# Three moves in a gated attention and recurrence block: an order written out for TensorE, eight copies on another engine, one unit's weight sums later

## The chip, the cores and the metric

The kernel runs on one core of a Trainium2 chip. The metric is the device time of one execution in microseconds (us), as the median of several runs. The profile is of one further execution, recorded by the hardware profiler. A core has a matrix engine, TensorE (PE), with its weight loads shown apart as PEld; VectorE (DVE), ScalarE (ACT) and GpSimd (POOL) for elementwise work; and SyncE (SP), which here only issues transfers. Each engine works through its own instructions in order, and waits at an instruction until what it needs is there.

## The reference

One layer, for 512 frames of 1024 values, in float32:

```python
xn = rmsnorm(x, norm_mix_g)
q, k, v, xr, gr, ga, gb = split(xn @ w_in)
ya = chunked_band_attention(q, k, v, rel_table) @ w_attn_out   # 16 heads of 64
yb = (rg_lru(causal_conv(xr)) * gelu(gr)) @ w_rnn_out
g_a, g_b = split(sigmoid([ga, gb] + b_merge))
h = x + (g_a * ya + g_b * yb) @ w_o
hn = rmsnorm(h, norm_ffn_g)
g, up = split(hn @ w_ffn_in)                                   # 2 x 2816 columns
h = h + (silu(g) * up) @ w_ffn_out
out = rmsnorm(h, final_norm_g)
```

The attention of a head adds a learned bias to the scores of earlier chunks, takes a softmax over them, and multiplies by v.

## The kernel before

**Matrix products.** A float32 operand is split into a high part, which ACT writes rounded to the matrix engine's type, and a low part, which DVE writes as the difference (`split`, lines 82 and 83). A product is then three matmuls (`mm3`, lines 76 to 78): high by high, high by low, low by high. Weights arrive by transfers that SP issues (`raw_...`, line 147) and are split into `whl_...`.

**Products by seven instead of eight.** Large products are grouped in units, in which sums and differences of weight blocks stand for one of eight block products. The sums of the blocks of w_ffn_out and w_o are made early, and parked in device memory: `spill` (lines 586 to 596) loads four blocks, makes four subtractions on DVE, the first line 591, and stores the results. `spill_of` does it for a unit, with buffers from a given pool. Unit 3's sums are made inside the loop over heads, after head 5 (`if h == 5`), in buffers of the pool `rnp`.

**Order.** The framework's scheduler chooses each engine's order from the program and from estimated costs, except in sections that `manual_schedule` covers for PE: there PE follows the program as written. The loop over heads is such a section. The stretch from the plain tiles of w_o to the first FFN tiles is not.

**Attention.** `scores` (lines 686 to 712) makes a head's scores (s), DVE adds the bias and takes the row extreme (line 707), ACT makes the exponentials with their row sums (708), DVE inverts the sums (`rl`, 709), POOL scales the four tiles of probabilities p (711). PE transposes p in the next step of the head loop (722) and uses it (742). POOL also casts the keys' low part, `kl` (656).

**After the attention.** The `ya` loop multiplies the attention's output by w_attn_out in eight tiles, `po_ya0` to `po_ya7`, 24 matmuls each; two tiles share one pair of weight loads, `raw_ya`, and splits, `whl_ya`.

**The plain tiles of w_o and the FFN norm.** Eight tiles `po_h` (four blocks t of 128 frames, two halves cc of the columns) get their last products in a loop over t. After each, DVE adds it into h (line 933) and ACT squares it for the norm (935). `norm_half` (339 to 360) then takes two blocks t: it scales them (`xs`, line 345), has PE transpose them in groups of two columns' tiles (`pt_ffn`, line 353), and writes from each transposed tile the high part `hn` (ACT, 357), the low part (DVE, 358) and a float copy `x` (ACT, 360), which later sums need. `first` are the first four FFN tiles, `po_f0` to `po_f3`, from the weights `fg0` and `fu0`; `project_half` makes one half of the frames of one of them. `weight_sums` prepares sums of FFN weights (`s_fg`, `s_fu`) and their splits on the same engines in the same stretch.

Of the kernel before, what the change touches and what calls it, by code (L numbers as in the profile page):

```python
# [36 lines left out]
def block_kernel(ctx: ExitStack, tc: tile.TileContext, x, norm_mix_g, w_in, b_merge, rel_table,  # L37
# [3 lines left out]
    pe, dve, act, pool, sp = nc.tensor, nc.vector, nc.scalar, nc.gpsimd, nc.sync  # L41
# [26 lines left out]
    def f(ap):  # L68
        return ap.bitcast(F32)

    def mm_tile(name, tag="mm"):
        return ps.tile([P, S], F32, tag=tag, bufs=4 if tag == "mm" else 2, name=name)

    def mm3(o, sh, sl, mh, ml, start, stop, parts=False):

        pe.matmul(o, sh, mh, start=start, stop=False, skip_group_check=parts)  # L76
        pe.matmul(o, sh, ml, start=False, stop=False, skip_group_check=parts)  # L77
        pe.matmul(o, sl, mh, start=False, stop=stop, skip_group_check=parts)  # L78
# [49 lines left out]
    front, units = (0, 1, 10), ((2, 3), (4, 5), (6, 7), (8, 9))  # L128
# [116 lines left out]
    def weights(name, ahead=1):  # L245
        prefetch(index[name] + 1 + ahead)
        return made[index[name]]
# [58 lines left out]
    ident = cp.tile([P, P], F32, name="ident")  # L306
# [3 lines left out]
    warm = cp.tile([P, 1], F32, name="warm")  # L310
# [28 lines left out]
    def norm_half(pl, src, ssq, g, dst, half, name, whole_of=None, then=None):  # L339
        xs = []  # L340
        for i in range(2):
            t = 2 * half + i
            rs = rstd(ssq[t], f"{name}{t}")
            xsc = pl.tile([P, D], F32, tag="xs", bufs=2, name=f"xs_{name}{t}")
            dve.tensor_scalar(xsc[:], src[t][:], rs[:, 0:1], None, ALU.mult)
            xs.append(xsc)
        if then:
            act.activation(warm[:], rs[:], then)
        for jp in range(0, KT, 2):
            pt = ps.tile([P, 2, 256], F32, tag="t", bufs=2, name=f"pt_{name}{half}_{jp}")  # L350
            for i in range(2):
                for j in range(2):
                    pe.transpose(pt[:, j, i * P:(i + 1) * P], xs[i][:, (jp + j) * P:(jp + j + 1) * P], ident[:])
            for j in range(2):
                jj = jp + j
                hi, lo = dst(jj, 0, half), dst(jj, 1, half)
                act.activation(hi, pt[:, j], AF.Identity, scale=g[:, jj:jj + 1])  # L357
                dve.scalar_tensor_tensor(lo, pt[:, j], g[:, jj:jj + 1], f(hi), ALU.mult, ALU.subtract)
                if whole_of:
                    act.activation(whole_of(jj, half), pt[:, j], AF.Identity, scale=g[:, jj:jj + 1])  # L360

    def features(pl, tag, name):

# [222 lines left out]
    def spill(w, unit, to, r):  # L586

        for n in range(4):
            sp.dma_start(out=r[n], in_=square(w, unit[n // 2], n % 2))
        b11, b12, b21, b22 = r  # L590
        dve.tensor_sub(b11, b12, b11)
# [190 lines left out]
    with tc.manual_schedule(engines={mybir.EngineType.PE}):  # L782
        for h in range(HEADS):
            pp = transposed(h, prob)
            if h + 1 < HEADS:
                prob = scores(h + 1)
            before, after = laid[h].split("|")
            project_all(before)
            weigh(h, pp)
            project_all(after)  # L790
            if h == 5:
                r = [rnp.tile([P, 2, 2, S], F32R, tag="big", bufs=4, name=f"spill3_{n}") for n in range(2)]
                spill(w_ffn_out, units[3], sums_d[3], [f(t[:, i]) for t in r for i in range(2)])
    aw2_stack.close()
    wo_stack, wop = opened("wo", 4)

# [39 lines left out]
    for j in range(KT):  # L836
        if j >= 4:
            wo_part(*blocks_wo[j - 4])
        py = mm_tile(f"po_ya{j}")
        project(py, weights(f"ya{j - j % 2}"), j % 2, aT)  # L840
        dve.scalar_tensor_tensor(ta[j], ta[j], 1.0, py[:], ALU.add, ALU.mult)
        dve.tensor_add(ta[j], ta[j], zB[j])
        at = lo_half if j < 2 else slice(0, S)
        split(mT[j][:, 0, at], mT[j][:, 1, at], ta[j][:, at])
        if j == 3:
            m_sum("s1")
            m_split("s1", m32("22"), m_at(0, hi_half))
            for name in ("s2", "s4", "s3"):
                m_sum(name)
# [66 lines left out]
    def hn_at(k, part, half):  # L916
        return bl[k // 4, half][:, part, k % 4]
# [1 line left out]
    hsq = []  # L919
    act.activation(warm[:], eps_t[:], AF.Sqrt)  # L920
    weight_sums("fg2", True)
    for t in range(NT):
        q2 = cp.tile([P, 2], F32, tag="hsq2", bufs=2, name=f"hsq2_{t}")
        for cc in range(2):
            po = bank_of(t, cc)
            for i in (2, 3):
                w = wo[f"wo{i}_{cc}"]
                for k in range(2):
                    mk = mT[2 * i + k]
                    mm3(po[:], mk[:, 0, t * P:(t + 1) * P], mk[:, 1, t * P:(t + 1) * P], w[:, 0, k], w[:, 1, k],  # L930
                        (t > 1 and cc == 1) and i == 2 and k == 0, k == 1, parts=True)
            hs = ht[t][:, cc * S:(cc + 1) * S]
            dve.scalar_tensor_tensor(hs, po[:], 0.5, hs, ALU.mult, ALU.add)
            junk = tg_.tile([P, S], F32, tag="tg", name=f"hj{t}_{cc}")
            act.activation(junk[:], hs, AF.Square, accum_out=q2[:, cc:cc + 1])
        q = cp.tile([P, 1], F32, tag="ssq", bufs=4, name=f"hsq{t}")
        dve.tensor_reduce(q[:], q2[:], mybir.AxisListType.X, ALU.add)
        hsq.append(q[:])
        if t == 1:
            norm_half(x32p, ht, hsq, gf, hn_at, 0, "ffn", f_at)  # L940
    wo_stack.close()
    xn_stack.close()

# [16 lines left out]
    def project_half(o, whl, c, half):  # L960
        at = slice(c * P, (c + 1) * P)
        for k in range(KT):
            mm3(o[:, half * 256:half * 256 + 256], whl(0, k, at), whl(1, k, at),
                hn_at(k, 0, half), hn_at(k, 1, half), k == 0, k == KT - 1)

    first = [mm_tile(f"po_f{i}") for i in range(4)]
    for i, name in enumerate(("fg0", "fg0")):
        project_half(first[i], weights(name), i % 2, 0)
    norm_half(x32p, ht, hsq, gf, hn_at, 1, "ffn", f_at, AF.Silu)
    for i, name in enumerate(("fu0", "fu0")):  # L970
        project_half(first[2 + i], weights(name, 0), i % 2, 0)


    def sums(name):
        t = acp.tile([P, 4, 256], F32, tag="act", name=f"sum_{name}")
# [28 lines left out]
    prefetch(index["fg2"] + 1)  # L1004

    for i, name in enumerate(("fg0", "fg0", "fu0", "fu0")):
        project_half(first[i], weights(name, 0), i % 2, 1)
    act0 = act_tile(0)
    for c in range(2):
        tg = swiglu_gate(first[c], c)  # L1010
# [239 lines left out]
```

## Time and profile before

| what | value |
|---|---|
| runs | 870.02, 870.34, 869.25 us; median 870.02 |
| profiled execution | 871.76 us, of which span 869.9 |
| PE busy | 852.9 us, 98% |
| DVE, ACT, POOL busy | 620.0, 505.3, 103.0 us |
| mean granted TensorE clock | 0.995 |
| the unit sums' loads (line 589) | 16, landing after 2.7, 5.8, 9.5 us (least, median, most) |

The span is from the first to the last instruction; the execution's time is 1.9 us longer. A row of a timeline gives the start, the length, the engine, the line and the operation, its result and its operands, and in brackets how long the engine idled before it and what ended the idling. A matmul's length overlaps the next one's: what counts is the distance between starts. A row of windows gives each engine's busy time in a stretch, and the granted clock as a share of full speed.

### The profile page before, as it was taken

To read this page: it belongs to the slowest core of one execution; us is meant where nothing else is said; L and a number is where in the kernel's file an instruction comes from. 1 tells how busy PE (TensorE), PEld (TensorE's weight loads), DVE (VectorE), ACT (ScalarE), POOL (GpSimd) and SP (SyncE) were. 2 spreads that over 40 slices of the span, in tenths; PEclk is the share of its full clock that TensorE was granted. 3 is DMA by queue.
4 is the path that set the end of the run, shared out by engine and by line. 5 is a ranking of instruction groups with operands and counts; after the bars stand their busy time and mean duration, and the time that the engine had idled before them with its cause. 6 is when DMAs were issued, how large, how long until landed. Compare 5 with 4: busy or idle time off the path is not lost.

```text
span 869.9 us, 12990 instructions
## 1 busy us (share of the span) xinstructions
PE 852.9 (98%) x4908; PEld 747.2 (86%) x4908; DVE 620.0 (71%) x952; ACT 505.3 (58%) x870; POOL 103.0 (12%) x135
## 2 busy tenths in 40 slices
PE   8999999999999998999999999999999999999996
PEld 5977887888888887888888889999999999988885
DVE  5789776636666658556568955898787887399973
ACT  7577687641466655666544446666555556284544
POOL 2013312200122315223200000000000001000011
PEclk9999999999999999999999999999999999999998
DMA  8585323339842246222146620343333233295602
GB/s 270 184 301 170 97 73 109 117 104 348 265 132 64 73 132 220 73 88 96 49 149 213 207 78 7 121 123 101 105 111 122 98 97 98 74 316 170 194 22 96
DMA packets 93870, 118.91 MB, mean 137 GB/s; under 512 B 6256, under 2 KB 71392, under 8 KB 93808
## 3 DMA queue, kind: packets, MB, share of 16 engines
q1 hardware_dynamic: 90128, 110.42, 39.1%
q10 hardware_dynamic: 3680, 7.67, 2.9%
q8 instruction: 38, 0.62, 0.3%
q14 instruction: 24, 0.20, 0.1%
HBM read 105.45 MB, written 12.62 MB: 136 GB/s over the span
## 4 chain that ended last, share of the span: by engine, by line
PE 93%; DVE 2%; ACT 2%; issue 1%; DMA 1%; POOL 1%; ACTq 0%; DVEq 0%; POOLq 0%
PE po_out L76 4%; PE po_out L78 4%; PE po_out L77 4%; PE p_fu L78 2%; PE p_fg L77 2%; PE p_fg L76 2%; PE p_fu L77 2%; PE p_fg L78 2%; PE p_fu L76 2%; PE o L742 2%; PE pT L722 2%; PE po_ga L76 2%; PE po_v L76 2%; PE po_ga L78 2%; PE po_v L78 2%; PE po_ya L76 2%
## 5 line engine op out<-in xcount | busy, mean ns | idle before, releaser
L711 POOL TENSOR_SCALAR p<-p,rl 128x128 f32<-128x128 f32 (+1 forms) x64 | 44.6, 716 | 162.9 <-DVE rl L709 162.8
L708 ACT ACTIVATE p<-p,m 128x128 f32<-128x128 f32 (+1 forms) x64 | 35.8, 561 | 16.0 <-DVE m L707 16.0
L1020 POOL TENSOR_TENSOR act_lo<-act,act_hi 128x1024 fp32r<-128x1024 f32 x1 | 2.4, 2407 | 301.2 <-DVE s_fu L175 301.2
L83 DVE TENSOR_TENSOR pp<-pT,pp 128x384 fp32r<-128x384 f32 (+1 forms) x48 | 27.8, 595 | 10.3 <-ACT pp L82 10.2
L707 DVE CUSTOM_DVE_ANT_0 p<-s,bias 128x128 f32<-128x128 f32 (+1 forms) x64 | 29.2, 482 | 3.9 <-PE s L704 3.8
L83 DVE TENSOR_TENSOR whl_qk<-raw_qk,whl_qk 128x1024 fp32r<-128x1024 f32 x16 | 21.7, 1354 | 10.9 <-ACT whl_qk L82 10.9
L76 PE MATMUL po_gr<-xnT,whl_gr 128*128 128x512 f32 (+1 forms) x80 | 28.1, 352 | 0.1
L83 DVE TENSOR_TENSOR whl_fu_s<-s_fu,whl_fu_s 128x1024 fp32r<-128x1024 f32 x20 | 24.2, 1223 | 5.3 <-ACT whl_fu_s L82 5.3
L82 ACT ACTIVATE whl_fg_s<-s_fg 128x1024 fp32r<-128x1024 f32 x20 | 20.9, 1055 | 12.1 <-PE q_fg L78 5.3
L77 PE MATMUL po_xr<-xnT,whl_xr 128*128 128x512 f32 (+1 forms) x80 | 27.8, 353 | 0.0
L77 PE MATMUL po_gr<-xnT,whl_gr 128*128 128x512 f32 (+1 forms) x80 | 27.8, 348 | 0.0
L78 PE MATMUL po_gr<-xnT,whl_gr 128*128 128x512 f32 (+1 forms) x80 | 27.5, 348 | 0.0
L78 PE MATMUL po_xr<-xnT,whl_xr 128*128 128x512 f32 (+1 forms) x80 | 27.3, 346 | 0.0
L76 PE MATMUL po_xr<-xnT,whl_xr 128*128 128x512 f32 (+1 forms) x80 | 26.7, 352 | 0.6 <-ACT xnT L357 0.6
L83 DVE TENSOR_TENSOR whl_fg_s<-s_fg,whl_fg_s 128x1024 fp32r<-128x1024 f32 x20 | 24.2, 1222 | 4.1 <-ACT whl_fg_s L82 4.1
L83 DVE TENSOR_TENSOR whl_t<-raw_t,whl_t 128x1024 fp32r<-128x1024 f32 x20 | 24.4, 1219 | 2.0 <-ACT whl_t L82 1.8
L82 ACT ACTIVATE whl_qk<-raw_qk 128x1024 fp32r<-128x1024 f32 x16 | 16.8, 1053 | 15.3 <-PE po_yb L78 8.8
L76 PE MATMUL po_gb<-xnT,whl_gb 128*128 128x512 f32 x64 | 25.1, 393 | 0.5 <-DVE sp_p L449 0.3
L76 PE MATMUL po_ga<-xnT,whl_ga 128*128 128x512 f32 x64 | 25.3, 395 | 0.0
L77 PE MATMUL po_gb<-xnT,whl_gb 128*128 128x512 f32 x64 | 25.2, 394 | 0.0
L78 PE MATMUL po_gb<-xnT,whl_gb 128*128 128x512 f32 x64 | 25.0, 391 | 0.0
L76 PE MATMUL po_q<-xnT,whl_qk 128*128 128x512 f32 x64 | 25.0, 391 | 0.0
(402 smaller groups left out, 3235.3 us busy)
## 6 DMA issues: line engine op xcount, KB each, us to landing
raw_fg<-in_w_ffn_in_dram SPq DMA_DIRECT2D x24, 512.0 KB, 3.5
raw_fu<-in_w_ffn_in_dram SPq DMA_DIRECT2D x22, 512.0 KB, 3.5
spill<-in_w_ffn_out_dram SPq DMA_DIRECT2D x16, 512.0 KB, 6.7
sums<-spill SPq DMA_DIRECT2D x16, 512.0 KB, 3.3
raw_qk<-in_w_in_dram SPq DMA_DIRECT2D x32, 256.0 KB, 3.7
raw_t<-sums SPq DMA_DIRECT2D x16, 512.0 KB, 4.0
raw_b<-in_w_ffn_out_dram SPq DMA_DIRECT2D x12, 512.0 KB, 4.4
raw_xr<-in_w_in_dram SPq DMA_DIRECT2D x8, 512.0 KB, 4.7
```

The source lines that it names most:

```text
L76: pe.matmul(o, sh, mh, start=start, stop=False, skip_group_check=parts)
L77: pe.matmul(o, sh, ml, start=False, stop=False, skip_group_check=parts)
L78: pe.matmul(o, sl, mh, start=False, stop=stop, skip_group_check=parts)
L82: act.activation(hi, src, AF.Copy)
L83: dve.tensor_sub(lo, src, f(hi))
L707: dve.tensor_tensor_reduce(prob[qb][:], scs[qb], bias[:, S - w:S], -1.0, 3e38, ALU.add, ALU.min, nmax[:, qb:qb + 1])
L708: act.activation(prob[qb][:], prob[qb][:], AF.Exp, bias=nmax[:, qb:qb + 1], scale=-1.0, accum_out=lsum[:, qb:qb + 1])
L711: pool.tensor_scalar(prob[qb][:], prob[qb][:], rl[:, qb:qb + 1], 1.0, ALU.mult, ALU.mult)
L722: pe.transpose(pt[:, at * P:(at + 1) * P], prob[qb][:, kb * P:(kb + 1) * P], ident[:])
L742: pe.matmul(po[:, S - n:S], st, pp[i][:, part, lo:lo + n], start=kb == 0 and part == 0, stop=kb == NT - 1 and part == 1)
L1020: (pool if i == 0 else dve).tensor_sub(lo[:], o[:], f(hi[:]))
```

## The change

Three things change.

1. Unit 3's sums leave the head loop. They are now issued in the `ya` loop, ahead of tile j = 5, through `spill_of` with buffers of the pool `aw`.
2. From the plain tiles of w_o to the first FFN tiles' first half, PE gets a `manual_schedule` section. `norm_half` is taken apart into `scaled` and `turned`; the groups of transposes stand at written places between the plain tiles and between the halves of the first FFN tiles. `project_half` becomes `project_part`, which can make a part of the sum over k.
3. In `turned`, every second float copy is written by DVE instead of ACT: eight of sixteen.

```diff
+    def scaled(pl, src, ssq, name, t):
+        rs = rstd(ssq[t], f"{name}{t}")
+        xsc = pl.tile([P, D], F32, tag="xs", bufs=2, name=f"xs_{name}{t}")
+        dve.tensor_scalar(xsc[:], src[t][:], rs[:, 0:1], None, ALU.mult)
+        return xsc, rs
+
+    def turned(xs, jp, g, dst, half, name, whole_of=None):
+        pt = ps.tile([P, 2, 256], F32, tag="t", bufs=2, name=f"pt_{name}{half}_{jp}")
...
+            act.activation(hi, pt[:, j], AF.Identity, scale=g[:, jj:jj + 1])
+            dve.scalar_tensor_tensor(lo, pt[:, j], g[:, jj:jj + 1], f(hi), ALU.mult, ALU.subtract)
+            if whole_of and j == 0:
+                act.activation(whole_of(jj, half), pt[:, j], AF.Identity, scale=g[:, jj:jj + 1])
+            elif whole_of:
+                dve.tensor_scalar(whole_of(jj, half), pt[:, j], g[:, jj:jj + 1], None, ALU.mult)
...
-            if h == 5:
-                r = [rnp.tile([P, 2, 2, S], F32R, tag="big", bufs=4, name=f"spill3_{n}") for n in range(2)]
-                spill(w_ffn_out, units[3], sums_d[3], [f(t[:, i]) for t in r for i in range(2)])
...
+        if j == 5:
+            spill_of(3, aw, "v", 8)
...
-        if t == 1:
-            norm_half(x32p, ht, hsq, gf, hn_at, 0, "ffn", f_at)
...
+    def project_part(o, name, c, half, ks):
+        at = slice(c * P, (c + 1) * P)
+        whl = weights(name, 0)
+        for k in ks:
+            mm3(o[:, half * 256:half * 256 + 256], whl(0, k, at), whl(1, k, at),
+                hn_at(k, 0, half), hn_at(k, 1, half), k == 0, k == KT - 1)
...
+    with tc.manual_schedule(engines={mybir.EngineType.PE}):
+        xs = []
+        for t in range(2):
+            for cc in range(2):
+                for i in (2, 3):
+                    plain_h(t, cc, i)
+                finish_h(t, cc)
+            xs.append(scaled(x32p, ht, hsq, "ffn", t)[0])
+        weights("fg0")
+        for cc, i in ((0, 2), (0, 3), (1, 2)):
+            plain_h(2, cc, i)
+        finish_h(2, 0)
+        for jp in (0, 2):
+            turned(xs, jp, gf, hn_at, 0, "ffn", f_at)
+        plain_h(2, 1, 3)
+        finish_h(2, 1)
+        for jp, i in ((4, 2), (6, 3)):
+            plain_h(3, 0, i)
+            turned(xs, jp, gf, hn_at, 0, "ffn", f_at)
+        finish_h(3, 0)
+        xs = [scaled(x32p, ht, hsq, "ffn", 2)[0]]
+        for i in (2, 3):
+            plain_h(3, 1, i)
+        finish_h(3, 1)
+        xs3, rs = scaled(x32p, ht, hsq, "ffn", 3)
+        xs.append(xs3)
+        for name, c in (("fg0", 0), ("fg0", 1), ("fu0", 0), ("fu0", 1)):
+            first.append(mm_tile(f"po_f{len(first)}"))
+            project_part(first[-1], name, c, 0, ends[0])
+            if (name, c) == ("fg0", 1):
+                for jp in (0, 2):
+                    turned(xs, jp, gf, hn_at, 1, "ffn", f_at)
+            if (name, c) == ("fu0", 0):
+                turned(xs, 6, gf, hn_at, 1, "ffn", f_at)
+                act.activation(warm[:], rs[:], AF.Silu)
+            project_part(first[-1], name, c, 0, ends[1])
+            if (name, c) == ("fg0", 1):
+                turned(xs, 4, gf, hn_at, 1, "ffn", f_at)
...
-    first = [mm_tile(f"po_f{i}") for i in range(4)]
-    for i, name in enumerate(("fg0", "fg0")):
-        project_half(first[i], weights(name), i % 2, 0)
-    norm_half(x32p, ht, hsq, gf, hn_at, 1, "ffn", f_at, AF.Silu)
-    for i, name in enumerate(("fu0", "fu0")):
-        project_half(first[2 + i], weights(name, 0), i % 2, 0)
```

In the rows of each engine's order below, a name ends in a number of the build, which differs between the two kernels; lines after 339 move by up to 37.

DVE's order at head 6 of the attention, before:

```order
L83 TENSOR_TENSOR aT_2909<-oacc_2732,aT_2909 128x512
L83 TENSOR_TENSOR whl_ga_0_3032<-raw_ga_0_3030,whl_ga_0_3032 128x1024
L591 TENSOR_TENSOR spill_0_2912<-spill_0_2912 128x1024
L709 RECIPROCAL rl_2953<-l_2951 128x4
L654 TENSOR_TENSOR kl_3008<-po_k_2982,kh_3007 64x512
L83 TENSOR_TENSOR whl_ga_4_3037<-raw_ga_4_3035,whl_ga_4_3037 128x1024
L744 TENSOR_TENSOR oacc_3017<-o_3018,oacc_3017 64x512
L592 TENSOR_TENSOR spill_0_2912<-spill_1_2913,spill_0_2912 128x1024
```

And DVE's order there in the changed kernel:

```order
L83 TENSOR_TENSOR aT_2909<-oacc_2732,aT_2909 128x512
L83 TENSOR_TENSOR whl_ga_0_3018<-raw_ga_0_3016,whl_ga_0_3018 128x1024
L712 RECIPROCAL rl_2939<-l_2937 128x4
L657 TENSOR_TENSOR kl_2994<-po_k_2968,kh_2993 64x512
L83 TENSOR_TENSOR whl_ga_4_3023<-raw_ga_4_3021,whl_ga_4_3023 128x1024
L747 TENSOR_TENSOR oacc_3003<-o_3004,oacc_3003 64x512
```

The subtractions of the spilled sums are gone; the reciprocal `rl` now follows the split of `whl_ga` at once.

SP's order of transfers from the second `ya` pair on, in the changed kernel (before, the rows of lines 592 and 599 are not there, and the others stand in the same order):

```order
L147 DMA raw_ya_0_4153<-in_w_attn_out_dram 128x4x256
L147 DMA raw_ya_4_4158<-in_w_attn_out_dram 128x4x256
L592 DMA spill_0_4275<-in_w_ffn_out_dram 128x2x512
L592 DMA spill_1_4276<-in_w_ffn_out_dram 128x2x512
L592 DMA spill_2_4277<-in_w_ffn_out_dram 128x2x512
L592 DMA spill_3_4278<-in_w_ffn_out_dram 128x2x512
L804 DMA raw_b_4226<-in_w_o_dram 128x2x512
L599 DMA sums_0_454<-spill_0_4275 128x1024
L599 DMA sums_2_456<-spill_1_4276 128x1024
L147 DMA raw_ya_0_4232<-in_w_attn_out_dram 128x4x256
L599 DMA sums_1_455<-spill_3_4278 128x1024
L147 DMA raw_ya_4_4237<-in_w_attn_out_dram 128x4x256
```

The four loads stand ahead of a load of w_o's block, and three of the four stores ahead of or between the two loads of the last `ya` pair.

DVE's order around the second half's last groups of transposed tiles, before (`hn` rows of line 358 are low parts):

```order
L997 TENSOR_TENSOR bt_4957<-sum_t_4945,bt_4957 128x1024
L358 SCALAR_TENSOR_TENSOR hn_4551<-pt_ffn_4_4875,vc,hn_4551 128x256
L358 SCALAR_TENSOR_TENSOR hn_4551<-pt_ffn_6_4886,vc,hn_4551 128x256
L83 TENSOR_TENSOR whl_fg_s_4983<-s_fg_4562,whl_fg_s_4983 128x2x512
L83 TENSOR_TENSOR whl_fu_a_5104<-raw_fu_0_5094,whl_fu_a_5104 128x512
L83 TENSOR_TENSOR whl_fu_a_5104<-raw_fu_4_5096,whl_fu_a_5104 128x512
L175 TENSOR_TENSOR s_fu_5099<-raw_fu_0_5094 128x512
L176 TENSOR_TENSOR s_fu_5099<-raw_fu_4_5096,s_fu_5098 128x512
L358 SCALAR_TENSOR_TENSOR hn_4551<-pt_ffn_4_4875,vc,hn_4551 128x256
L358 SCALAR_TENSOR_TENSOR hn_4551<-pt_ffn_6_4886,vc,hn_4551 128x256
```

And in the changed kernel, where line 354 is the low part and 358 the float copy:

```order
L354 SCALAR_TENSOR_TENSOR hn_4553<-pt_ffn_4_4868,vc,hn_4553 128x256
L1034 TENSOR_TENSOR bt_4962<-sum_t_4950,bt_4962 128x1024
L354 SCALAR_TENSOR_TENSOR hn_4553<-pt_ffn_4_4868,vc,hn_4553 128x256
L358 TENSOR_SCALAR x_2_4556<-pt_ffn_4_4868,vc 128x256
L354 SCALAR_TENSOR_TENSOR hn_4553<-pt_ffn_6_4892,vc,hn_4553 128x256
L1020 TENSOR_TENSOR sum_t_4951<-x_2_4556,sum_t_4950 128x512
L1020 TENSOR_TENSOR sum_t_4952<-x_2_4556,x_0_4554 128x512
L1020 TENSOR_TENSOR sum_t_4953<-x_2_4556,sum_t_4951 128x512
L354 SCALAR_TENSOR_TENSOR hn_4553<-pt_ffn_6_4892,vc,hn_4553 128x256
L358 TENSOR_SCALAR x_3_4557<-pt_ffn_6_4892,vc 128x256
```

Between the low parts of these two groups there now stand sums of the float copies, and no weight splits or weight sums.

More of the change, by code (lines that the diff above doesn't have):

```diff
@@ L337, in rstd @@
         return rs
-    def norm_half(pl, src, ssq, g, dst, half, name, whole_of=None, then=None):
-        xs = []
-        for i in range(2):
[L342 to L348, printed above, removed]
-        for jp in range(0, KT, 2):
[L350 to L360, printed above, removed]
@@ new lines, in scaled @@
+    def scaled(pl, src, ssq, name, t):
[5 more added lines that the diff above has]
+        pt = ps.tile([P, 2, 256], F32, tag="t", bufs=2, name=f"pt_{name}{half}_{jp}")
+        for i in range(2):
+            for j in range(2):
+                pe.transpose(pt[:, j, i * P:(i + 1) * P], xs[i][:, (jp + j) * P:(jp + j + 1) * P], ident[:])
+        for j in range(2):
+            jj = jp + j
+            hi, lo = dst(jj, 0, half), dst(jj, 1, half)
+            act.activation(hi, pt[:, j], AF.Identity, scale=g[:, jj:jj + 1])
[4 more added lines that the diff above has]
+                dve.tensor_scalar(whole_of(jj, half), pt[:, j], g[:, jj:jj + 1], None, ALU.mult)
@@ L362, in features, with norm_half @@
+    def norm_half(pl, src, ssq, g, dst, half, name):
+        xs = [scaled(pl, src, ssq, name, 2 * half + i)[0] for i in range(2)]
+        for jp in range(0, KT, 2):
+            turned(xs, jp, g, dst, half, name)
     def features(pl, tag, name):
@@ L921, in block_kernel @@
     weight_sums("fg2", True)
[L922 to L938, printed above, removed]
-        if t == 1:
-            norm_half(x32p, ht, hsq, gf, hn_at, 0, "ffn", f_at)
+    q2s = {}
@@ new lines, in plain_h, with finish_h @@
+    def plain_h(t, cc, i):
+        w = wo[f"wo{i}_{cc}"]
+        for k in range(2):
+            mk = mT[2 * i + k]
+            mm3(bank_of(t, cc)[:], mk[:, 0, t * P:(t + 1) * P], mk[:, 1, t * P:(t + 1) * P], w[:, 0, k], w[:, 1, k],
+                (t > 1 and cc == 1) and i == 2 and k == 0, k == 1, parts=True)
+    def finish_h(t, cc):
+        if t not in q2s:
+            q2s[t] = cp.tile([P, 2], F32, tag="hsq2", bufs=2, name=f"hsq2_{t}")
+        hs = ht[t][:, cc * S:(cc + 1) * S]
+        dve.scalar_tensor_tensor(hs, bank_of(t, cc)[:], 0.5, hs, ALU.mult, ALU.add)
+        junk = tg_.tile([P, S], F32, tag="tg", name=f"hj{t}_{cc}")
+        act.activation(junk[:], hs, AF.Square, accum_out=q2s[t][:, cc:cc + 1])
+        if cc:
+            q = cp.tile([P, 1], F32, tag="ssq", bufs=4, name=f"hsq{t}")
+            dve.tensor_reduce(q[:], q2s[t][:], mybir.AxisListType.X, ALU.add)
+            hsq.append(q[:])
@@ new lines, in project_part @@
+    def project_part(o, name, c, half, ks):
[4 more added lines that the diff above has]
+                hn_at(k, 0, half), hn_at(k, 1, half), k == 0, k == KT - 1)
+    first = []
+    ends = range(0, KT // 2), range(KT // 2, KT)
+    with tc.manual_schedule(engines={mybir.EngineType.PE}):
[36 more added lines that the diff above has]
+                turned(xs, 4, gf, hn_at, 1, "ffn", f_at)
@@ L958, in swiglu_gate @@
         return tg
[L960 to L964, printed above, removed]
-    first = [mm_tile(f"po_f{i}") for i in range(4)]
-    for i, name in enumerate(("fg0", "fg0")):
-        project_half(first[i], weights(name), i % 2, 0)
-    norm_half(x32p, ht, hsq, gf, hn_at, 1, "ffn", f_at, AF.Silu)
-    for i, name in enumerate(("fu0", "fu0")):
-        project_half(first[2 + i], weights(name, 0), i % 2, 0)
     def sums(name):
@@ L1006, in block_kernel @@
     for i, name in enumerate(("fg0", "fg0", "fu0", "fu0")):
-        project_half(first[i], weights(name, 0), i % 2, 1)
+        project_part(first[i], name, i % 2, 1, range(KT))
     act0 = act_tile(0)
```

## The prediction

> **What bounds the kernel now.** I read the page's busy times and chain first, then the windows of the stretches where TensorE is not full, then the timelines of the engines around those stretches.
>
> ```profile
> span 869.9 us, 12990 instructions
> PE 852.9 (98%) x4908; PEld 747.2 (86%) x4908; DVE 620.0 (71%) x952; ACT 505.3 (58%) x870; POOL 103.0 (12%) x135
> PE 93%; DVE 2%; ACT 2%; issue 1%; DMA 1%; POOL 1%; ACTq 0%; DVEq 0%; POOLq 0%
> ```
>
> TensorE (PE) is busy 98% of the span and holds 93% of the chain that ended last. The change removes no matmul, so all it can give is time in which PE stands, or runs slowly, at places it touches. Two ten-microsecond windows in mid-kernel are not full. In window rows the first number pair is the stretch, then its length, then PE, PEld, DVE, ACT and POOL busy, then the granted clock, DMA share and GB/s.
>
> ```profile
> 330.00:340.00 10.00, 7.44 (x38) 5.78 (x37) 8.71 (x18) 5.85 (x14) 5.26 (x6) 1.00 0.57 218
> 540.00:550.00 10.00, 7.44 (x51) 7.03 (x49) 9.28 (x16) 7.04 (x14) 0.00 (x0) 0.86 0.18 52
> 542.70:546.20 3.50, 0.94 (x7) 0.60 (x5) 3.50 (x7) 1.91 (x6) 0.00 (x0) 1.00 0.01 1
> 547.20:550.40 3.20, 3.20 (x17) 3.20 (x16) 3.20 (x7) 2.15 (x3) 0.00 (x0) 0.50 0.30 106
> ```
>
> Call the first hole A (head 6 of the attention) and the second hole C (first FFN tiles). Hole C is followed by 3.20 us at clock 0.50.
>
> **Hole A, and what the moved sums cost.** PE, start and length:
>
> ```profile
> 330.15 0.27 PE L722 MATMUL pT<-ident,p 128*128 128x128 f32 x1
> 330.96 0.33 PE L722 MATMUL pT<-ident,p 128*128 128x128 f32 x1 [0.53 <-POOL p L711]
> 331.52 0.33 PE L722 MATMUL pT<-ident,p 128*128 128x128 f32 x1 [0.23 <-POOL p L711]
> 333.15 0.98 PE L722 MATMUL pT<-ident,p 128*128 128x128 f32 x7 [1.30 <-POOL p L711]
> 333.89 0.30 PE L703 MATMUL s<-kh,q 128*128 128x128 f32 x1
> 334.68 0.33 PE L704 MATMUL s<-kl,q 128*128 128x128 f32 x1 [0.49 <-POOL kl L656]
> ```
>
> The seven transposes from 333.15 take 0.74 us to the next start, 0.106 each. Ten of them from 330.15 would take 1.06; they take 3.74. That is 2.68 lost. From 333.89 to 334.68 one matmul takes 0.79 instead of 0.11: 0.68 more. Hole A is worth 3.36 us. All ten transposes wait for the probabilities p that POOL scales, and POOL had been waiting for one small VectorE (DVE) instruction:
>
> ```profile
> 322.79 0.19 ACT L708 ACTIVATION_READ_ACCUMULATOR p<-p,m 128x1 f32 x1
> 325.81 1.23 DVE L591 TENSOR_TENSOR spill<-spill 128x1024 f32<-128x1024 f32 x1 [2.27 <-DMA spill<-in_w_ffn_out_dram]
> 326.95 0.17 DVE L709 RECIPROCAL rl<-l 128x4 f32<-128x4 f32 x1
> 327.31 5.78 POOL L711 TENSOR_SCALAR p<-p,rl 128x128 f32<-128x128 f32 x4 [17.79 <-DVE rl L709]
> 333.16 1.47 POOL L656 CAST kl<-kl 64x512 fp32r<-64x512 f32 x1
> ```
>
> The row sums were there at 322.98 (322.79 + 0.19), yet the reciprocal ran at 326.95: the first subtraction of spill 3 stands ahead of it in DVE's queue and stood 2.27 us for its loads. In the new order no spill instruction stands there, and the reciprocal follows the split of whl_ga. That split ended at 323.5 (325.81 − 2.27), so the reciprocal comes 3.4 us earlier. POOL's four scalings then run from about 323.9 to 329.7, done before PE asks at 330.15; the kl cast behind them ends near 331.2 (329.7 + 1.47), and PE, 2.68 us earlier at the scores, wants it at about 331.3 (334.68 − 3.36). So all of A goes, less a residue of 0 to 0.3; I take 0.2.
>
> The sums reappear after the attention: 4 loads on SP, 4 subtractions on DVE, 4 stores on SP. The loads wait until PE has finished the last o, because their buffers are those of the attention:
>
> ```profile
> 436.11 0.28 PE po_ya L76
> 439.82 0.23 PE po_ya L77
> L591 DVE TENSOR_TENSOR spill<-spill,spill x3: 1209/1226/1226, 41.1 to 215.1; 128x1024 f32<-128x1024 f32 x3
> DMA to landing us min/median/max: 2.7/5.8/9.5
> 450.00:460.00 10.00, 10.00 (x46) 8.29 (x45) 7.20 (x11) 5.13 (x7) 0.00 (x0) 1.00 0.60 197
> 470.00:480.00 10.00, 10.00 (x45) 8.26 (x44) 6.29 (x9) 2.52 (x4) 0.00 (x0) 1.00 0.44 153
> ```
>
> Loads issued at about 436.3 land by 445.8 at the worst seen (9.5), and four subtractions at 1.23 make 4.9 us of DVE. DVE has 2.8 us free in 450 to 460 and 3.7 in 470 to 480. What queues behind them on DVE is the second split of the weights of the third ya pair (whl_ya4), which PE wants four tiles after 436.11. The chain's rows from 436.11 to 439.82 are 16 matmuls, 0.23 each; a tile is 24 of them, 5.5 us, so PE is there at about 458. With the worst landing the split comes at about 451, some 7 us early. On SP the stores stand among the loads of the last pair (raw_ya6), wanted split two tiles later, at 469; they would be issued by 456 and split by about 460. Nothing of it reaches PE: cost 0. It is hidden by PE's ya tiles. Without that cover it costs its lateness: each microsecond of landing beyond about 16.5 us after the issue (9.5 + 7) would be one of PE time. Bounds: 0 and, at the landing times seen, 0.
>
> **Hole C, and the written order.** PE, then DVE:
>
> ```profile
> 502.90 0.39 PE L77 MATMUL po_h<-whl_wo,mT 128*128 128x512 f32 x1
> 503.13 0.39 PE L78 MATMUL po_h<-whl_wo,mT 128*128 128x512 f32 x1
> 539.96 0.60 PE L353 MATMUL pt_ffn<-ident,xs_ffn 128*128 128x128 f32 x4
> 542.55 0.28 PE L78 MATMUL po_f<-hn,whl_fu 128*128 128x256 f32 x1
> 543.84 0.50 PE L76 MATMUL po_f<-hn,whl_fg 128*128 128x256 f32 x2 [1.01 <-ACT hn L357]
> 546.13 0.38 PE L77 MATMUL po_f<-hn,whl_fg 128*128 128x256 f32 x1 [1.55 <-DVE hn L358]
> 548.06 0.41 PE L77 MATMUL po_f<-hn,whl_fu 128*128 128x256 f32 x1
> 548.27 0.41 PE L78 MATMUL po_f<-hn,whl_fu 128*128 128x256 f32 x1
> 542.05 1.22 DVE L83 TENSOR_TENSOR whl_fg_s<-s_fg,whl_fg_s 128x1024 fp32r<-128x1024 f32 x1 [0.46 <-ACT whl_fg_s L82]
> 543.19 1.28 DVE L83 TENSOR_TENSOR whl_fu_a<-raw_fu,whl_fu_a 128x512 fp32r<-128x512 f32 x2
> 544.40 0.68 DVE L175 TENSOR_TENSOR s_fu<-raw_fu 128x512 f32<-128x512 f32 x1
> 545.60 0.87 DVE L358 SCALAR_TENSOR_TENSOR hn<-pt_ffn,vc,hn 128x256 fp32r<-128x256 f32 x2
> ```
>
> The last transposes of the second half come at 539.96, 2.6 us before PE runs out of other matmuls. The last low parts (L358 at 545.60) stand on DVE behind a weight split, two more and the fu sums. PE's steps: 542.55 to 543.84 is 1.29 for one matmul of 0.12, so 1.17 lost; 543.84 to 546.13 is 2.29 for four, 1.81 lost. Then the pitch is 0.21 instead of 0.12 for 3.20 us, 15 matmuls that would take 1.80: 1.40 lost. Hole C is worth 4.38 us; A and C together 7.74.
>
> The written order keeps the matmuls and moves the transposes. In before's clock it parts from the old one at 502.90, among the plain tiles. I count along it with 0.23 for a matmul of 128x512 (502.90 to 503.13), 0.12 for one of 128x256 and 0.106 for a transpose. Counted so, it puts the last two groups of second-half transposes at about 531.6 and 533.5, between the first half of fu0's first tile and its second, instead of 539.17 and 539.96. The first matmul on their results then stands at about 538.4, five microseconds behind the last transposes. ACT and DVE need for one group's two high and low parts 4 × 0.48 = 1.9 us, with the copies 2.9:
>
> ```profile
> L358 DVE SCALAR_TENSOR_TENSOR hn<-pt_ffn,vc,hn x16: 471/476/486, 519.9 to 546.0; 128x256 fp32r<-128x256 f32 x16
> L360 ACT ACTIVATE x<-pt_ffn,vc x16: 455/476/492, 520.7 to 546.5; 128x256 f32<-128x256 f32 x16
> 511.94 0.75 DVE L345 TENSOR_SCALAR xs_ffn<-h,rs_ffn 128x1024 f32<-128x1024 f32 x1
> 530.00:540.00 10.00, 10.00 (x87) 10.00 (x86) 4.23 (x8) 5.63 (x13) 0.00 (x0) 1.00 0.01 2
> ```
>
> The last low part then comes near 538.3, and its matmul stands at about 541.2. It is tightest at the start: first transposes at 513.6 (47 plain matmuls from 502.90) against xs ready at 512.69 (511.94 + 0.75), 0.9 to spare; the third group (jp 4), whose PSUM tile waits for the copies out of the first, is ready by my count at 517.45 against 517.14, a stall of 0.3; and the second half's xs of tile 3 about 526.8 against 526.9, 0 to 0.2. I take 0.3 for the order.
>
> Eight float copies go from ACT to DVE. No such copy stands on DVE in this trace; the nearest rows bound it: a quarter of the 0.75 us scaling of 128x1024 (0.19) and the low part from PSUM (0.48). That is 1.5 to 3.8 us of DVE in a stretch where it idles 5.8 of 10 (530 to 540). I take 0.39 each, 3.1 us, off PE's path: 0. If it were on the path, it would show as the third group's stall, which contains one copy.
>
> Sum: 3.36 − 0.2 + 4.38 − 0.3 = 7.2 us. The profiled execution took 871.76 (span 869.9, 1.9 around it); it would become 864.5. The median of the runs is 1.7 lower, 870.02, and becomes **862.8 us**.
>
> **The clock, weighed.** In this trace hole A (four waits, 2.55 us of idling within 4.5) left the clock at 1.00, and hole C (1.01 + 1.55 within 3.5, PE busy 0.94) was followed by 0.50. By these rows a denser stretch keeps 1.00, so the 1.40 goes with C. [...]
>
> **Rivals.**
> - R1, the written order stalls in its turn. PE now waits in program order: behind a transposition that isn't ready stand all later matmuls, where the scheduler's order had others to put in. For it: slacks of 0.9, −0.3 and 0.1 us above. Against: DVE is at 42% in 530 to 540. If 4.4 us come back, only A is gained: 870.02 − 3.2 = 866.8.
> - R2, hole A stays, because POOL's 5.78 us of scalings or the kl cast end late anyway (the cast's margin is only 0.1 us). Only C: 870.02 − 4.1 = 865.9. Against: the reciprocal's release moves by 3.4 us.
> - R3, the slow clock has another cause than the idling, and stays: 862.8 + 1.4 = 864.2. For it: hole A idled as much without a drop.
> - R4, slower than before. The moved loads land late, and DVE, in order, stands at the first subtraction with the ya splits behind it. PE starts to wait at a landing of 16.5 us after the issue; 7.2 us more only eat the gain; from about 25.5 us the time exceeds 871.8. At 27 us it is 873.3. For it: four 512 KB loads come in one piece beside the ya loads, and DMA is at 0.60 there. Against: 9.5 is the longest landing seen.
>
> **How the numbers follow.** Forecast 0.66, R1 0.12, R2 0.10, R3 0.07, R4 0.05. The forecast's own range is 861.0 to 864.5 (7.7 all gone and 0.6 of scatter each way, by the runs' 869.25 to 870.34; residues up to 1.0). The range takes in R1, R2 and R3: 861.0 to 867.2. A measurement of this kernel tells about 0.2% (1.7 us) from no change. All but R4 and a mixture of R1 with R2 lie below 868.3: faster 0.90, same 0.05, slower 0.05.
>
> **What would show it.** In the changed profile: the window 330 to 340 with PE at 9.5 or more, the reciprocal directly behind a whl_ga split, POOL's scalings ending before the first transpose of that head. In the ya stretch PE full in each window, four subtractions between 440 and 460. From 500 to 550 PE full and no row with clock below 1.00; if a gap stands at the third group of transposes it should be about 0.3. Wrong would be: PE waiting on DVE or ACT anywhere in 503 to 550 for more than 1 us in sum (R1), POOL still the releaser at 330 (R2), clock 0.50 without a hole (R3), or PE waiting for whl_ya (R4).

## The result, and the profile after

The changed kernel takes 864.04 us (863.91 to 864.16, 4 runs) beside 869.83 us for the kernel before (869.25 to 870.34, 4 runs). The ratio is 0.9934, with a 95% interval of 0.9916 to 0.9951: a gain of 5.8 us, between 4.3 and 7.3. The forecast was 862.8 in a range of 861.0 to 867.2. Direction and range held; the gain is 1.4 us smaller than the sum. The profiled spans, 869.9 and 862.4, differ by 7.5 us, which is more than the runs do. That gap is what the experiments are about. One execution of the kernel before, at 1053.55 us and a mean granted clock of 0.752, stands far from all others and is in none of the figures below.

The page of the changed kernel, and its windows at the places of the two holes and of the moved sums (the columns are those of the windows before):

```profile
span 862.4 us, 12989 instructions
PE 850.9 (99%) x4908; PEld 745.6 (86%) x4908; DVE 620.8 (72%) x960; ACT 501.7 (58%) x862; POOL 98.2 (11%) x135
330.00:340.00 10.00, 10.00 (x56) 8.69 (x54) 7.16 (x17) 7.72 (x17) 3.70 (x6) 1.00 0.14 41
442.00:452.00 10.00, 10.00 (x46) 8.29 (x45) 9.97 (x12) 3.02 (x5) 0.00 (x0) 1.00 0.85 297
510.00:520.00 10.00, 9.72 (x55) 8.09 (x54) 7.61 (x17) 7.83 (x20) 0.00 (x0) 1.00 0.18 54
520.00:530.00 10.00, 9.96 (x84) 9.73 (x84) 7.64 (x17) 5.96 (x13) 0.00 (x0) 1.00 0.01 2
540.00:550.00 10.00, 10.00 (x85) 10.00 (x85) 10.00 (x14) 6.65 (x11) 0.00 (x0) 1.00 0.50 159
```

PE is full where hole A and hole C were, and the clock is 1.00 in each of these windows. What remains in the changed stretch is a small loss between 510 and 530. At head 6 and in the ya tiles the timelines of DVE and POOL show:

```profile
322.24 1.23 DVE L83 TENSOR_TENSOR whl_ga<-raw_ga,whl_ga 128x1024 fp32r<-128x1024 f32 x1
323.38 0.17 DVE L712 RECIPROCAL rl<-l 128x4 f32<-128x4 f32 x1
323.75 2.06 POOL L714 TENSOR_SCALAR p<-p,rl 128x128 f32<-128x128 f32 x4 [14.46 <-DVE rl L712]
439.30 1.23 DVE L594 TENSOR_TENSOR spill<-spill,spill 128x1024 f32<-128x1024 f32 x1 [2.91 <-DMA spill<-in_w_ffn_out_dram]
447.76 1.22 DVE L597 TENSOR_TENSOR spill<-spill,spill 128x1024 f32<-128x1024 f32 x1
449.50 1.22 DVE L83 TENSOR_TENSOR whl_ya<-raw_ya,whl_ya 128x1024 fp32r<-128x1024 f32 x1
```

The reciprocal follows the split of whl_ga at once, as forecast (323.5). POOL's four scalings take 2.06 us, not the 5.78 of before; I had left them at 5.78. In the ya tiles the four subtractions run between 439.30 and 449.0, and the split that I expected at 451 starts at 449.50, while PE stays full.

In the written order PE waits at one place, and loses a little more at a second:

```profile
514.08 0.63 PE L349 MATMUL pt_ffn<-ident,xs_ffn 128*128 128x128 f32 x4 [0.28 <-ACT hj L939]
523.43 1.29 PE L349 MATMUL pt_ffn<-ident,xs_ffn 128*128 128x128 f32 x8
```

Measured from start to start against the usual distance for the shape, 0.56 us go between 510 and 520, at the third group of transposes, and 0.24 between 520 and 530, at the first groups of the second half. The second of the two scaled tiles `xs` that these transpose is ready at 523.79 (DVE, 523.04 + 0.75), 0.36 behind the start of the transposes at 523.43. I had taken 0.3 for the first and 0 to 0.2 for the second.

Below, "loss" of a stretch always means this: the sum, over PE's matmuls, of the distance to the next start less the median distance for that shape. By it, the profiled execution of the kernel before lost 3.47 us in 320 to 340 (hole A) and 4.71 in 540 to 560 (hole C with what follows).

### The profile page after: what moved, and what is told of

Read it like the earlier page. It is cut to its first block, busy times and chain, and to the rows that moved or that the text cites. A ratio compares the mean times of both kernels' runs of the same rounds, so it can differ in the third digit from the quotient of the medians.

```text
span 862.4 us, 12989 instructions
## 1 busy us (share of the span) xinstructions
PE 850.9 (99%) x4908; PEld 745.6 (86%) x4908; DVE 620.8 (72%) x960; ACT 501.7 (58%) x862; POOL 98.2 (11%) x135
## 4 chain that ended last, share of the span: by engine, by line
PE 95%; ACT 1%; DVE 1%; issue 1%; DMA 1%; SPq 0%; DVEq 0%; ACTq 0%
PE po_out L76 4%; PE po_out L77 4%; PE po_out L78 4%; PE o L745 2%; PE p_fg L78 2%; PE p_fg L77 2%; PE p_fg L76 2%; PE p_fu L78 2%; PE p_fu L77 2%; PE p_fu L76 2%; PE pT L725 2%; PE po_ga L76 2%; PE po_v L76 2%; PE po_ga L78 2%; PE po_q L76 2%; PE po_ya L76 2%
## 5 line engine op out<-in xcount | busy, mean ns | idle before, releaser
L714 POOL TENSOR_SCALAR p<-p,rl 128x128 f32<-128x128 f32 (+1 forms) x64 | 39.6, 638 | 166.4 <-DVE rl L712 166.3
```

The costliest lines, as they stand in the source:

```text
L714: pool.tensor_scalar(prob[qb][:], prob[qb][:], rl[:, qb:qb + 1], 1.0, ALU.mult, ALU.mult)
```

## The experiments

**What do executions of the kernel before share?** The gap between runs and spans suggested that something in the one profiled execution was not typical. My first suspect was the slow clock behind hole C. The kernel is unchanged, so there is no edit.

> The unchanged kernel once more, to see what its executions share. The changed kernel gained 5.8 us in the runs, 7.6 in the profiled spans. Theory D: the stretch at clock 0.50 behind hole C (1.4 us) belongs to the one profiled execution, not to the kernel; most executions will have a mean clock of 0.997 or more, spans near 868.1, times of 869.3 to 870.4, and a profile of such a one shows hole C with 2.9 to 3.0 us lost and no clock of 0.50 behind it. Theory N: the slow stretch is in every execution (mean clock 0.995 each, the window 547 to 551 at 0.50), and the missing 1.4 to 1.8 us are new stalls of the changed kernel.

Measured: 869.24 us (868.55 to 873.02, 11 runs), ratio 0.9997 (0.9982 to 1.0011) to the runs beside it. Theory D fell as the account of the gap, though not in favour of N. This profiled execution took only 868.58, with clock 0.995 and its window 540 to 550 at 0.83: the slow clock behind hole C is there again. (N fell too: the mean clocks of the 11 runs are 0.995 to 0.997, so the slow stretch is not in all of them alike.) What is missing is hole A.

```profile
330.00:340.00 10.00, 9.78 (x54) 8.41 (x53) 9.78 (x18) 6.33 (x16) 3.21 (x3) 1.00 0.57 222
540.00:550.00 10.00, 7.80 (x50) 7.60 (x51) 9.85 (x17) 7.17 (x13) 0.00 (x0) 0.83 0.33 100
324.96 1.23 DVE L591 TENSOR_TENSOR spill<-spill 128x1024 f32<-128x1024 f32 x1 [1.61 <-DMA spill<-in_w_ffn_out_dram]
326.10 0.17 DVE L709 RECIPROCAL rl<-l 128x4 f32<-128x4 f32 x1
326.47 3.45 POOL L711 TENSOR_SCALAR p<-p,rl 128x128 f32<-128x128 f32 x4 [17.28 <-DVE rl L709]
329.47 1.51 DVE L592 TENSOR_TENSOR spill<-spill,spill 128x1024 f32<-128x1024 f32 x1 [0.89 <-DMA spill<-in_w_ffn_out_dram]
```

The reciprocal is still late, at 326.10, but POOL needs only 3.45 us for the four scalings, and is done at 329.9, before PE asks at about 330. The loss in hole A is 0.49 us. DVE idled 0.89 ahead of its second subtraction, waiting for the load.

Three further executions of the same kernel, each profiled, tested whether hole A is what makes its executions differ.

> A further look at the unchanged kernel. If hole A alone makes its executions differ, then time less the loss in hole A is the same in each: 871.76 - 3.47 = 868.3 and 868.58 - 0.49 = 868.1 so far, and 868.1 with the sums moved. Expected: time = 868.2 + A, within 0.4, and A large (over 2.5) where GpSimd's four scalings take over 5 us, small (under 1) where they take under 4. Rival: executions differ elsewhere (start, hole C, clock), and time less A scatters by over 1 us.

> A second further look at the unchanged kernel; as the first: time = 868.2 + A, within 0.4; rival: time less A scatters by over 1 us.

> A third further look at the unchanged kernel; as the first: time = 868.2 + A, within 0.4; rival: time less A scatters by over 1 us.

| execution of the kernel before | time | DVE's wait at L591 | POOL's four scalings | loss in hole A | time less the loss |
|---|---|---|---|---|---|
| the profile of the prediction | 871.76 | 2.27 | 5.78 | 3.47 | 868.3 |
| the one above | 868.58 | 1.61 | 3.45 | 0.49 | 868.1 |
| first further one | 868.58 | 1.64 | 4.40 | 0.75 | 867.8 |
| second further one | 872.68 | 2.19 | 5.78 | 4.39 | 868.3 |
| third further one | 872.79 | 2.35 | 5.78 | 4.63 | 868.2 |

Five executions, and time less the loss is 867.8 to 868.3. Hole A has a small form and a large one. In these five the large one comes with a wait of 2.19 us or more and with scalings of 5.78; the first further one, with 4.40, lies between my two bounds and belongs to the small form. The third one's rows:

```profile
330.00:340.00 10.00, 7.77 (x33) 6.14 (x32) 8.72 (x17) 4.86 (x13) 5.28 (x6) 0.83 0.58 217
325.82 1.23 DVE L591 TENSOR_TENSOR spill<-spill 128x1024 f32<-128x1024 f32 x1 [2.35 <-DMA spill<-in_w_ffn_out_dram]
327.33 5.78 POOL L711 TENSOR_SCALAR p<-p,rl 128x128 f32<-128x128 f32 x4 [17.86 <-DVE rl L709]
333.17 1.35 PE L722 MATMUL pT<-ident,p 128*128 128x128 f32 x7 [1.30 <-POOL p L711]
```

The median of the kernel before, 869.2 to 870.6 in the comparisons, is 868.1 plus 1.1 to 2.5: its runs hold middle values too, of which I have no profile.

**The sums alone.** From the kernel before:

```diff
-            if h == 5:
-                r = [rnp.tile([P, 2, 2, S], F32R, tag="big", bufs=4, name=f"spill3_{n}") for n in range(2)]
-                spill(w_ffn_out, units[3], sums_d[3], [f(t[:, i]) for t in r for i in range(2)])
...
+        if j == 5:
+            spill_of(3, aw, "v", 8)
```

> Only the sums of unit 3 are moved behind the attention; the order of the FFN norm is the old one. Hole A is worth 3.4 us by the trace, so both theories give 869.8 - 3.4 = 866.4 (866.0 to 866.8), and a window 330 to 340 with PE full. If the moved sums cost something in the ya tiles, it is less than that.

Measured: 868.11 us (867.92 to 868.67, 11 runs) beside 869.96 (23 runs); ratio 0.9976 (0.9966 to 0.9987). The window is full, as expected, but the time is 1.7 us above the expectation. Moving the sums is worth 2.1 us by the ratio (1.1 to 3.0), not 3.2. The runs of this kernel lie within 0.75 us; those of the kernel before reached from 868.41 to 874.87. The move takes away the scatter, down to what the shortest executions had anyway.

```profile
330.00:340.00 10.00, 10.00 (x55) 8.69 (x54) 7.46 (x17) 7.99 (x18) 3.79 (x6) 1.00 0.18 52
540.00:550.00 10.00, 8.45 (x56) 8.24 (x57) 9.85 (x16) 7.26 (x12) 0.00 (x0) 0.83 0.38 109
542.27 0.39 PE L77 MATMUL po_f<-hn,whl_fg 128*128 128x256 f32 x1 [1.55 <-DVE hn L358]
```

Hole C is untouched here: the same 1.55 us of waiting, and the clock at 0.83 over 540 to 550.

**The written order and the copies alone.** The changed kernel, with the sums put back:

```diff
+            if h == 5:
+                r = [rnp.tile([P, 2, 2, S], F32R, tag="big", bufs=4, name=f"spill3_{n}") for n in range(2)]
+                spill(w_ffn_out, units[3], sums_d[3], [f(t[:, i]) for t in r for i in range(2)])
...
-        if j == 5:
-            spill_of(3, aw, "v", 8)
```

> Only the written order and the copies on VectorE; unit 3's sums stay behind head 5. Theory D: the gaps of hole C without the slow clock are 3.0 us, the new stalls between 513 and 524 take 0.8, so 869.8 - 2.2 = 867.6 (867.2 to 868.0). Theory N: 4.4 - 0.8, 866.2.

Measured: 866.49 us (865.31 to 868.42, 5 runs); ratio 0.9960 (0.9947 to 0.9973), a gain of 3.5 us (2.3 to 4.6). This interval holds both expectations, so it does not decide between them. The profiled execution, 868.42, has a large hole A again (loss 4.28, clock 0.83 in its window) and none at C:

```profile
330.00:340.00 10.00, 8.06 (x34) 6.44 (x33) 8.36 (x17) 5.25 (x13) 4.92 (x6) 0.83 0.56 218
540.00:550.00 10.00, 10.00 (x86) 10.00 (x85) 10.00 (x13) 8.44 (x11) 0.00 (x0) 1.00 0.32 101
```

Sharper is the distance between the kernel with the sums moved, 868.11, and the next one, which has everything but the copies on DVE, 864.13, timed side by side and both with little scatter: 4.0 us for the written order.

**All copies on ScalarE.** The changed kernel with

```diff
-            if whole_of and j == 0:
+            if whole_of:
                 act.activation(whole_of(jj, half), pt[:, j], AF.Identity, scale=g[:, jj:jj + 1])
-            elif whole_of:
-                dve.tensor_scalar(whole_of(jj, half), pt[:, j], g[:, jj:jj + 1], None, ALU.mult)
```

> The changed kernel with all sixteen float copies on ScalarE. By my forecast the eight copies cost nothing on VectorE and it is 864.0 as well (863.7 to 864.3). Rival: in the written order ScalarE, 7.8 of 10 busy from 510 to 520, releases the transposes' PSUM tiles, and four more copies of 0.36 in the first half delay the third group by 0.4 to 1.0: 864.4 to 865.0. Rival the other way: the copy on VectorE is what the third group waits for, and the 0.56 lost there shrinks: 863.5.

Measured: 864.13 us (863.99 to 865.15, 5 runs), ratio 0.9936 (0.9923 to 0.9949), beside the changed kernel's 0.9934. The copies on DVE give and cost nothing that shows in the time (864.04 and 864.13, not timed side by side). The trace still shows the rival at work: the third group now waits for a copy on ACT, and loses 0.90 instead of 0.56; but the 0.24 at the second half's start are gone, so the sum is 0.9 instead of 0.8.

```profile
514.11 0.66 PE L349 MATMUL pt_ffn<-ident,xs_ffn 128*128 128x128 f32 x4 [0.58 <-ACT x L356]
```

**Is a late reciprocal enough for hole A?** From the kernel before, for unit 3 only:

```diff
         dve.tensor_sub(b11, b12, b11)
-        dve.tensor_sub(b12, b22, b12)
-        dve.tensor_sub(b22, b22, b11)
-        dve.tensor_sub(b21, b21, b22)
+        if whole:
+            dve.tensor_sub(b12, b22, b12)
+            dve.tensor_sub(b22, b22, b11)
+            dve.tensor_sub(b21, b21, b22)
```

> The kernel before with three of unit 3's four subtractions left out (the sums it stores are wrong in three of four blocks; loads, stores and the first subtraction, with its wait, stay). It tells two readings of hole A apart. Reading P (place alone): the reciprocal is late behind the waiting subtraction, and that makes the hole; it stays, 3 us at a wait of 2.0 us or more, and the median is 869 to 870. Reading B (both): a late reciprocal is not enough, the hole needs VectorE's dense subtractions beside GpSimd's scalings too, which then take 5.8 us instead of 2 to 3; without them the scalings end by 330.2 whatever the wait, hole A is 0 to 0.6, and the time is that of the kernel with the sums moved, 868.1 (867.7 to 868.7).

Measured: 868.52 us (868.01 to 869.19, 11 runs) beside 870.56 (16 runs); ratio 0.9975 (0.9964 to 0.9986). Reading B holds. The wait is there, and the reciprocal is as late as in the prediction's profile, yet the hole is a loss of 0.34:

```profile
325.68 1.23 DVE L591 TENSOR_TENSOR spill<-spill 128x1024 f32<-128x1024 f32 x1 [2.19 <-DMA spill<-in_w_ffn_out_dram]
326.82 0.17 DVE L710 RECIPROCAL rl<-l 128x4 f32<-128x4 f32 x1
327.19 3.43 POOL L712 TENSOR_SCALAR p<-p,rl 128x128 f32<-128x128 f32 x4 [17.83 <-DVE rl L710]
327.49 1.20 DVE L83 TENSOR_TENSOR whl_ga<-raw_ga,whl_ga 128x1024 fp32r<-128x1024 f32 x1
330.00:340.00 10.00, 9.93 (x55) 8.38 (x54) 6.83 (x17) 7.93 (x18) 5.27 (x10) 1.00 0.70 253
```

In the prediction's profile POOL's four scalings, from 327.31 to 333.09, had these three instructions of DVE on 128x1024 beside them from start to end:

```profile
327.61 1.21 DVE L83 TENSOR_TENSOR whl_ga<-raw_ga,whl_ga 128x1024 fp32r<-128x1024 f32 x1
329.35 1.21 DVE L592 TENSOR_TENSOR spill<-spill,spill 128x1024 f32<-128x1024 f32 x1
331.31 1.23 DVE L593 TENSOR_TENSOR spill<-spill,spill 128x1024 f32<-128x1024 f32 x1
```

POOL takes 3.43 us when the three later subtractions are absent, and 5.78 when two of them, and the first half microsecond of the third, run beside it with no idle time of DVE between them. The surplus over 2.06 (the time in the changed kernel, and at 259.85 in the kernel before, where DVE is idle beside it) is about the time of the DVE instructions on 128x1024 that ran beside from start to end: 2.06 + 1.20 = 3.26 against 3.43 here, and 2.06 + 1.21 + 1.21 + 1.23 = 5.71 against 5.78. DVE's shorter instructions there (0.65 to 0.69) are not in these sums, and in the changed kernel one of 0.69 and the first 0.69 of a split stood beside the 2.06. That the scalings are slower beside DVE's instructions on 128x1024 is what these rows show; by what path, they don't. Nor was it tested by itself whether the subtractions make the hole when the reciprocal is on time: in the small form the reciprocal comes 0.8 to 1.0 us earlier and the second subtraction waits for its load, both at once.

**Two pieces of the written order, later.** The changed kernel with

```diff
-        for jp, i in ((4, 2), (6, 3)):
+        for i in (2, 3):
             plain_h(3, 0, i)
+        for jp in (4, 6):
             turned(xs, jp, gf, hn_at, 0, "ffn", f_at)
...
             project_part(first[-1], name, c, 0, ends[0])
+            rest = ends[1]
             if (name, c) == ("fg0", 1):
+                project_part(first[-1], name, c, 0, rest[:1])
+                rest = rest[1:]
...
-            project_part(first[-1], name, c, 0, ends[1])
+            project_part(first[-1], name, c, 0, rest)
```

> The changed kernel with two pieces of the written order put later: the third group of first-half transposes behind both products of tile (3, 0), and the first two groups of the second half three matmuls later. The trace of the changed kernel loses 0.56 at the third group and 0.24 at the second half's first. If these waits are only a matter of place, both go and it is 864.0 - 0.8 = 863.2 (863.0 to 863.6). Rival: the low parts of the first half come later by as much, and the first FFN tile waits for them: 864.0 or more.

Measured: 863.60 us (863.40 to 863.88, 5 runs), ratio 0.9916 (0.9900 to 0.9931). PE waits at neither place any more, but pauses at a new one:

```profile
515.20 1.03 PE L349 MATMUL pt_ffn<-ident,xs_ffn 128*128 128x128 f32 x8
523.50 1.04 PE L349 MATMUL pt_ffn<-ident,xs_ffn 128*128 128x128 f32 x8
526.57 0.39 PE L77 MATMUL po_f<-hn,whl_fg 128*128 128x256 f32 x1
```

The matmul at 526.57 is the first on a low part of `hn` behind two on high parts that start at 526.16; 0.28 is lost there. So the loss between 520 and 530 stays, at 0.26, and moves from the transposes to the first use of their results: by its place a wait of the kind that the rival named, but in the second half; its row names no releaser. The 0.56 at the third group are gone. The time is 0.4 us below the changed kernel, with ranges that do not touch, though the two were not timed side by side. It is at the upper edge of what I expected, half of the 0.8; it is the fastest of the versions here.

**The cover of the moved sums.** The changed kernel with the sums made twice:

```diff
         if j == 5:
             spill_of(3, aw, "v", 8)
+            spill_of(3, aw, "v", 8)
```

> The changed kernel with unit 3's sums made twice in the ya tiles (the same loads, subtractions and stores again, 4.9 us more of VectorE and 4 MB more of transfers in 436 to 480). It measures the cover that I priced at nothing. By my count the splits of whl_ya were 4 to 7 us ahead of TensorE in the changed kernel, so most of it hides: 864.0 to 865.0. Rival: VectorE, 9.97 of 10 busy from 442 to 452 already, is the bound there, and all of it comes out on TensorE: 864.0 + 4.9 = 869.

Measured: 864.40 us (864.20 to 864.57, 6 runs), ratio 0.9925 (0.9909 to 0.9941). Four more loads, subtractions and stores cost about 0.4 us beside the changed kernel's 864.04 (not timed side by side); DVE is full from 466 to 486, and PE is full in all of 436 to 486:

```profile
446.00:456.00 10.00, 10.00 (x46) 8.28 (x45) 7.89 (x12) 2.25 (x4) 0.00 (x0) 1.00 0.99 352
466.00:476.00 10.00, 10.00 (x46) 8.29 (x45) 10.00 (x13) 4.35 (x5) 0.00 (x0) 1.00 0.71 265
```

The splits of whl_ya stand ahead of most of the second sums. The last pair's two come 3.3 and 1.4 us later than in the changed kernel, counted from the second subtraction, and PE does not wait for them. What is lost in addition stands behind the ya tiles: 0.84 instead of 0.56 between 510 and 520, of which 0.22 at the first transposes of the norm.

## Why the prediction was right, and where its sum was off

- **The moved sums cost nothing in the ya tiles.** Right: PE is full there, the loads landed within 7.7 us, and even twice the work leaves PE full there and costs about 0.4 later. Rival R4, slower than before, had no ground.
- **The written order removes hole C.** Right, and of the size in the sum: 4.38 less 0.3 was 4.1; the side-by-side distance is 4.0. Inside it, the new stalls were 0.8 rather than 0.3, at the two places that the prediction named as tight; rival R1 is these, and stayed small. Hole C with what follows was 4.7 rather than 4.4.
- **The copies at nothing.** Right: 864.13 without them.
- **Hole A at 3.36, less 0.2.** This is the term that was mis-sized. The measured worth of moving the sums is 2.1 us (1.1 to 3.0), 1.9 by the medians. The step that failed is the one that took a hole from one profiled execution, of 871.76, as the kernel's, and then set the sum against a median that lay 1.7 lower. The 1.7 were not something common to both kernels, as the subtraction treated them; they were that execution's large hole A. The five profiled executions lose 0.49 to 4.63 there and agree within 0.5 in what is left. Had I let the surplus of the profiled execution come off the hole, A would have been 3.2 − 1.7 = 1.5, and the forecast 870.0 − 1.5 − 4.1 = 864.4; that the surplus belonged to A and not to C is known only from the later executions. The measured 864.04 still lies in the forecast's own range of 861.0 to 864.5, which allowed for residues and scatter but not for a hole that varies. Read off one of the other four profiles, the same sum would have given anything from 861.5 to 865.7, so that it held is partly luck. (The lower bound, 861.0, is below its own terms: 870.02 − 7.74 − 0.6 is 861.7.)
- **The cause of hole A** was told only by half. The prediction has POOL waiting "for one small VectorE (DVE) instruction": the late reciprocal alone leaves a loss of 0.34, with three subtractions taken away. The row of 5.78 us for four instructions stood in the prediction, and the same four at other heads of the same trace read:

```profile
259.85 2.06 POOL L711 TENSOR_SCALAR p<-p,rl 128x128 f32<-128x128 f32 x4 [7.41 <-DVE rl L709]
269.29 3.03 POOL L711 TENSOR_SCALAR p<-p,rl 128x128 f32<-128x128 f32 x4 [7.07 <-DVE rl L709]
```

- **R3, a slow clock that has another cause,** did not come: in the five profiles without hole C the clock is 1.00 from 530 to 550, and in the changed kernel's from 500 to 560. But the clock term was not what I thought either. In the second further execution hole C is followed by clock 1.00 up to 560, and PE waits later instead:

```profile
540.00:550.00 10.00, 7.43 (x61) 7.03 (x60) 8.99 (x15) 6.56 (x14) 0.00 (x0) 1.00 0.15 52
550.00:560.00 10.00, 9.11 (x73) 8.51 (x71) 10.00 (x14) 7.48 (x12) 0.00 (x0) 1.00 0.52 158
558.14 0.38 PE L76 MATMUL p_fg<-bt,whl_fg_s 128*128 128x256 f32 x1 [0.74 <-ACT keepa_fg L277]
```

The loss of 540 to 560 is 3.07 + 1.65 = 4.72 there, and 4.39 + 0.32 = 4.71 in the prediction's profile with the slow clock. The ACT instruction named in the last row had itself waited for DVE (line 1011), and DVE, busy 10.00 of 10, is behind after hole C: from its low parts at 545.60 to its split at 558.32 it runs the same course in both profiles, 0.92 us later in this one. So PE loses the same whether it runs slowly or waits at the next place. The same holds for all seven profiles with hole C: they lose 4.6 to 4.9 between 530 and 560, four of them with the slow clock and three without. So the sum's 1.40 for the clock was right as a size and wrong as a cause: by these profiles, keeping the clock up alone would have given nothing.

## What to carry to other kernels

A hole that varies with the landing of a transfer is a distribution (hole A lost 0.49 to 4.63 us in five executions, in which DVE waited 1.61 to 2.35 for the load), and one profile shows one draw of it. When the profiled execution is above the median of the runs, take the surplus off the hole that can vary before summing; a second profile of the unchanged kernel can show which hole that is. And where an engine's instructions take longer than the same ones do elsewhere in the trace (POOL's scalings, 5.78 us against 2.06), ask which neighbour is running beside them: moving that neighbour can be part of the gain.

## What was not expected of the hardware

- POOL's four scalings of one head took 2.06 us with DVE idle beside them (259.85, in the profile of before), 3.03 with one DVE weight split of 128x1024 beside them (269.77 to 271.19, in the same profile), and 5.78 with a split and two subtractions beside them (327.31): 1.0 to 1.2 more for each such instruction, whose own length was 1.2 to 1.4. With one split beside them and three of the subtractions left out they took 3.43, 1.4 more. Shorter DVE instructions that ran beside are not counted in this.
- The granted clock fell behind holes in which the longest wait of PE that I read is 1.55 us: behind hole C in four of seven profiles (0.50 for 3.20 us in the prediction's, after waits of 1.01 and 1.55; 0.83 over 540 to 550 in each of the other three), and behind the large hole A in three of four: two of the three further executions and the kernel with the sums put back (the window's clock 0.83 in each, after waits of 0.6, 0.2 and 1.3 in the third further execution). Behind the other like holes it stayed at 1.00, at hole C after a wait of 1.56 in the second and the third further execution. What decides between the two outcomes was not shown.
